# A hybrid decoder layer on one core: one store per pair for the turned head outputs, and their weaving in four copies

## The chip, the core and the metric

The kernel runs as one program on one core of a Trainium2 chip. Its engines are PE (matmuls), DVE (VectorE), ACT (ScalarE), POOL (GpSimd) and SP, which here only issues DMAs. The metric is the device time of one execution in microseconds; the median of three runs before the change is 1531.04 us.

## The reference

One layer over 1024 rows of 1024 channels, in float32: a normalised input is projected to eight groups of 1024 channels, two token mixers run side by side, gates merge them, then an output projection and an MLP with squared ReLU follow. What the change touches is the second mixer's output `o` and where it meets its gates:

```python
h = rms_norm(x, norm_mix)
proj = h @ w_in
xa, ga, q, f, v, g, m_a, m_b = split(proj)               # eight groups of 1024
y_a = rg_lru(conv(xa), ...) * gelu(ga)
o = rms_norm(hgrn2_chunkwise(silu(q), kf, log_f, v), hg_norm)   # 8 heads of 128
y_b = o * silu(g)
y = sigmoid(m_a) * y_a + sigmoid(m_b) * y_b
x = x + y @ w_out
x = x + square(relu(rms_norm(x, norm_mlp) @ w_up)) @ w_down
return rms_norm(x, norm_final)
```

## The kernel before

**Stages.** The rows are worked on in two halves of 512 (c = 0, 1), the heads in four pairs (p = 0 to 3). First come the mixers, eight stages of (c, p), up to about 545 us. Then the gates: the channel groups g, m_b, ga and m_a, computed over all rows, up to about 815 us. Then the output projection, the MLP and the final norm. Every float32 factor is split into a rounded upper part H and a lower part L (`split`: a cast on ACT makes H, a subtraction on DVE makes L), and each product is three matmuls (`mm3`, L158), so that one product of 128x512 outputs over 512 channels is 12 matmuls.

**The head outputs.** In the mixers, `on` holds a stage's normalised outputs with rows on partitions. The DMA transposition works on 16-bit halves of the float32 words, so `onT` (`on_T`) comes out with the low and the high 16-bit halves of each number apart. It is stored to DRAM (`od[p]`, one tensor per pair), by ACT's DMA queue. In the gate stage `with_o(p)` loads the pair's `od` into `op` (L1281, one DMA of 128 partitions x 8 KB), puts the two halves back together with one copy on ACT (L1282, "weaving": it reads half-planes and writes them interleaved into `o`) and multiplies `g2`, the product of gates g and m_b, by the norm's gain and `o` on DVE (L1285).

**The gate stage.** It goes in quads: q = 4p + gate, gate 0 to 3 for g, m_b, ga, m_a; quads 0 and 1 are done in the mixers' last stage, so q runs from 2 to 15. Each quad multiplies two 2x2 blocks with seven products instead of eight; (q, s) below is step s of quad q. Steps 0, 2, 4, 6 go to a bank of PSUM called X, 1 and 5 to Y, 3 to Z. A step adds onto what its bank holds, and what the bank held must first be read out: after steps 0, 1, 2 by a copy on ACT (`ge`, L1209), after 3, 4, 5 by a sum on DVE (`gb`, L1212), after 6 by a copy on ACT (`gb`, L1214):

```python
        if step < 3:
            ge[q, step] = gp.tile([P, T], F32, tag="e", name=f"ge{step}_{q}", bufs=4)
            added[q, step] = A.copy(ge[q, step], o)
```

So (q, 2) waits for the copy of (q, 0), (q, 4) for that of (q, 2), (q, 5) for that of (q, 1), (q, 6) for the sum of (q, 4). Steps 3 to 6 of a quad read operands called B21, T3, B22, T4; T3 and T4 are made in the mixers, stored in DRAM (`cdT`) and loaded as H and L parts (`gT3H`, `gT3L`, `gT4H`, `gT4L`) by SP at the start of the stage (L1176). The first two quads are interleaved: (2,0), (2,3), (2,1), (2,2), (2,5), (2,4), (3,0), (2,6), then (3,1) to (3,6), (4,0) and so on. The weights of quad q are `q` tiles of number 32 + q, loaded two DMAs per quad (`load_quad`), summed on DVE (`s`, L1121 to L1130) and split into the pairs named wA11, ws1, ws3 and wA12 (`wA`, `ws136H` for quad 4, and so on).

**What sets the order.** The engines run their instructions in order. The order is made by a scheduler from the order of writing, priorities (`tc.high_priority`) and manual edges: `held(a, b)` puts a behind b without a wait across engines, and `added[q, s]` is the instruction that read out step s of quad q. `in_turn` issues a DMA on SP with high priority, behind the last one so issued. Each DMA of SP and ACT takes the next of eight semaphores (DMAHW0 to DMAHW7) and, where that one's last user has not landed, waits for it on its queue.

**The turned keys.** In a mixer stage (`hgrn`) the keys are turned on PE into the banks `pk`, copied by ACT into `kT` (L868), and PE's next product (`pkv`) reads them.

Of the kernel before, what the change touches and what calls it, by code (L numbers as in the profile page):

```python
# [15 lines left out]
ALU = mybir.AluOpType  # L16
# [3 lines left out]
P = 128  # L20
D = 1024
S = 1024
T = 512
# [18 lines left out]
PV_LB, PV_CB, PV_BR, PV_BI, PV_LAM, PV_CW, PV_HG = 0, 8, 16, 24, 32, 40, 72  # L42
# [4 lines left out]
def trunk(ctx: ExitStack, tc: tile.TileContext, x, wts, mlp, pv, gains, mask_f, mask_u, out):  # L47
    nc = tc.nc
    V, A, G, PE = nc.vector, nc.scalar, nc.gpsimd, nc.tensor
# [39 lines left out]
    def held(ins, behind, reason="order"):  # L89
        how = mybir.DependencyInfo(mybir.DependencyClass.NoSync, mybir.DependencyReason.DATA)  # L90
        tc.add_manual_dep(ins.ins, behind.ins.name, how, reason=reason)
        return ins
# [76 lines left out]
    pvt = const.tile([P, PV_N], F32, tag="pvt", name="pvt")  # L169
# [60 lines left out]
    od = [dram.tile([P, 2, 4 * T], U16, tag=f"od{p}", name=f"od{p}") for p in range(NPAIR)]  # L230
# [327 lines left out]
    def on_T(c, p, got, queue):  # L558
        t = mt("tmp", f"onT{c}{p}", (P, 2, T)).rearrange("p a b -> p (a b)").bitcast(U16)
        t = t.rearrange("p (j x) -> p j x", x=P)  # L560
        ins = queue.dma_start_transpose(t, got["on"].rearrange("p g j d -> p (g j d)").bitcast(U16))

        turned_on.append(ins)

        def stored(dma):
            for g in range(2):
                dst = od[p][64 * g : 64 * g + 64, :, 2 * c * T : 2 * (c + 1) * T]
                src = t[:, 8 * g : 8 * g + 8, :].rearrange("p j x -> p (j x)")
                dma(dst.rearrange("a h t -> (a h) t"), src)

        return stored

# [117 lines left out]
    def hgrn(c, p, got, go):  # L690
# [117 lines left out]
        for b in range(4):  # L808
# [5 lines left out]
                op0=ALU.mult,  # L814
                op1=ALU.add,
# [4 lines left out]
        for n in range(8):  # L820
            for b in (0, 2):
                k = 4 * n + b
# [33 lines left out]
        nkv = 3 if c + 1 == NC else 4  # L856
# [3 lines left out]
        pk = [bank("hg", f"pk{c}{u}") for _, u in both]  # L860
# [3 lines left out]
        kT = []  # L864
        kTs = mt("rr", f"kT{nm}", (P, 2, 4, P))
        for s, u in both:
            kT.append(kTs[:, s])
            A.copy(kT[s][:, :nkv, :], pk[s][:, : nkv * P].rearrange("p (n k) -> p n k", n=nkv))  # L868
        go(at[3])
        pkv = [bank("hg", f"pkv{c}{u}") for _, u in both]  # L870
        for s, _ in both:
# [4 lines left out]
        for s, u in both:  # L876
            sn = sns[:, s]
            states.append([scar[:, u, :]] + [sn[:, n, :] for n in range(4)])
            for n in range(nkv):
# [3 lines left out]
                else:  # L883
# [5 lines left out]
                        op0=ALU.mult,  # L889
                        op1=ALU.add,  # L890
# [294 lines left out]
    def behind_steps(ins):  # L1185
        how = mybir.DependencyInfo(mybir.DependencyClass.NoSync, mybir.DependencyReason.DATA)
        tc.add_manual_dep(ins.ins, added[own[1], 4].ins.name, how, reason="behind_steps")
# [37 lines left out]
    def gate_work(q):  # L1225
        p, gate = divmod(q, 4)
        b = gb.pop(q)
        if gate == 0:
            sg = gp_tile("sg", f"sg{q}")
            sigmoids(sg, b)  # L1230
            V.tensor_tensor(out=b, in0=sg, in1=b, op=ALU.mult)
            live["g2"] = b
        elif gate == 1:
            sigmoids(b, b)
            V.tensor_tensor(out=live["g2"], in0=live["g2"], in1=b, op=ALU.mult)
            with_o(p)
        elif gate == 2:
            t = gp_tile("sg", f"sg{q}")
            A.activation(t, b, AF.Square)
            ins = V.tensor_scalar(t, t, 0.044715, 1.0, op0=ALU.mult, op1=ALU.add)  # L1240
            if q == own[0]:
                behind_steps(ins)
            V.tensor_tensor(out=t, in0=t, in1=b, op=ALU.mult)
            for two in (slice(0, 2), slice(2, 4)):
                ins = A.activation(t[:, two, :], t[:, two, :], AF.Tanh, scale=GELU_C)
                if q == own[0]:
                    how = mybir.DependencyInfo(mybir.DependencyClass.NoSync, mybir.DependencyReason.DATA)
                    tc.add_manual_dep(ins.ins, added[own[2], 0].ins.name, how, reason="tanh")
            for cut, one in ((slice(0, 4, 3), 1.0), (slice(1, 3), -1.0)):
                V.scalar_tensor_tensor(b[:, cut, :], t[:, cut, :], one, b[:, cut, :], op0=ALU.add, op1=ALU.mult)  # L1250
            h = load_4(hd[p], f"h{p}")
            V.scalar_tensor_tensor(b, b, 0.5, h, op0=ALU.mult, op1=ALU.mult)
            live["g1"] = b
        else:
            g1, g2 = live.pop("g1"), live.pop("g2")
            last = p + 1 == NPAIR
            yh, yl = gp_tile("sg", f"yH{p}").bitcast(F32R), gp_tile("ld", f"yL{p}").bitcast(F32R)
            for c in range(NC):
                two = slice(2 * c, 2 * c + 2)
                for j in (2 * c, 2 * c + 1):  # L1260
                    A.activation(b[:, j, :], b[:, j, :], AF.Sigmoid, scale=SIGN[j])
                ins = V.tensor_tensor(out=b[:, two, :], in0=b[:, two, :], in1=g1[:, two, :], op=ALU.mult)
                if q == own[1]:
                    held(ins, added[own[2], 4])
                for j in (2 * c, 2 * c + 1):
                    op = ALU.add if p == 0 or SIGN[j] > 0 else ALU.subtract
                    ins = V.tensor_tensor(out=b[:, j, :], in0=b[:, j, :], in1=g2[:, j, :], op=op)
                    if q == own[1]:
                        how = mybir.DependencyInfo(mybir.DependencyClass.NoSync, mybir.DependencyReason.DATA)
                        tc.add_manual_dep(ins.ins, added[own[2], 4].ins.name, how, reason="sums of the next")  # L1270
                if last and c == 0:
                    split(b[:, two, :], yt[0][p][:, 0], yt[0][p][:, 1])
                else:
                    split(b[:, two, :], yh[:, two, :], yl[:, two, :])
                    for t, y in enumerate((yh, yl)):
                        nc.sync.dma_start(yd[p][:, t, two, :], y[:, two, :].bitcast(F32))

    def with_o(p):
        parts, o = gp_tile("ld", f"op{p}"), gp_tile("sg", f"o{p}")
        as_16 = lambda t: t.rearrange("p a b -> p (a b)").bitcast(U16)  # L1280
        nc.sync.dma_start(as_16(parts), od[p].rearrange("a h t -> a (h t)"))  # L1281
        A.copy(  # L1282
            as_16(o).rearrange("p (t h) -> p h t", h=2), as_16(parts).rearrange("p (h t) -> p h t", h=2)
        )
        ins = V.scalar_tensor_tensor(  # L1285
            live["g2"], live["g2"], pvt[:, PV_HG : PV_HG + 1], o, op0=ALU.mult, op1=ALU.mult
        )
        if p == 0:
            behind_steps(ins)

    yt = {}

# [39 lines left out]
    gwork[own[0]]["c"]()  # L1332
    live["g2"] = gp_tile("b", "g2_0")
    nc.sync.dma_start(live["g2"], g2d)
    for q in own:
        n = q + 1
        if n > own[1] and n < QUADS:
            gwork[n] = quad_steps(GQ + n, (w1p, wp), minus=True)
        for step in (1, 2, 5, 4, 6) if q == own[0] else (0, 1, 2, 3, 4, 5, 6):
            if q in own[1:3] and step == 0:  # L1340
                continue
            pinned[0] = q < own[2]
            gate_step(q, step)
            if q == own[0] and step == 4:
                gate_step(own[1], 0)
            if q == own[2] and step == 4:
                gate_work(own[1])
            if q == own[1] and step == 6:
                pinned[0] = False
                gate_step(own[2], 0)  # L1350
                with_o(0)
                gate_work(own[0])
            pinned[0] = False
            if n == QUADS:
                if step == 2:
                    close_np()
                    yp, close_yp = opened("yp", side="right")
                    y_tiles(yp, 0)
                    most[0] = len(seq)
                    fill_w(n_mix + 1)  # L1360
                if step == 5:
                    fill_w(n_mix + 3)
                continue
            if step == 1 and q > own[0]:
                load_quad(GQ + n, dma=in_turn if n == own[2] else nc.sync.dma_start)
            for k in {2: ("sums", "a", "b"), 5: ("c",), 6: ("d",)}.get(step, ()):
                if (q, k) == (own[1], "sums"):
                    gwork[n][k](rest_a12)
                elif q > own[0]:
                    gwork[n][k]()  # L1370
                elif k != "a":
                    with tc.high_priority(300):
                        done = gwork[n][k]()
                    if k == "d":
                        rest_a12 = done
        if q > own[1]:
            gate_work(q)
# [572 lines left out]
```

## Time and profile before

| what | value |
|---|---|
| three runs, us | 1527.86, 1531.04, 1532.47 |
| median, us | 1531.04 |
| profiled execution, us | 1529.59 |
| its span, us | 1527.8 |
| PE / DVE / ACT / POOL busy, us | 1514.5 / 1147.3 / 811.1 / 154.5 |
| granted PE clock, mean | 0.999 |
| weaving copies on ACT (L1282), count and mean us | 4, 4.84 |
| stores of onT (od), count and size | 16, 256 KB |
| loads of op, count and size | 4, 1024 KB |

The span runs from the first to the last instruction of the profiled execution; the time has a little more around it. Busy times of engines overlap. A row of a timeline gives start and duration in us, engine, line, operation, output<-input, and in brackets how long its engine stood idle before it and what ended that. A row of the waits gives who waited for whom, the total in us, how many times, and the longest.

### The profile page before, as it was taken

The numbers are of one execution on the slowest core, as the hardware profiler recorded it, in microseconds if no ns is written. First come the engines' busy times: TensorE is split into PE (matmuls) and PEld (weight loads), VectorE is DVE, ScalarE is ACT, GpSimd is POOL, SyncE is SP. The second block draws the span as 40 slices with busy tenths as digits, with TensorE's granted clock in tenths as the row PEclk, the third lists the DMA queues.
The fourth block names the chain that finished last, engine by engine and source line by source line (L and its number), as shares of the span: only waits on it lengthen the run. The fifth ranks groups of instructions, "written<-read, shape, count | busy, mean of one in ns | idle before, by whom it ended". The sixth has DMA issues, their size and how long they took to land.

```text
span 1527.8 us, 23130 instructions
## 1 busy us (share of the span) xinstructions
PE 1514.5 (99%) x9027; PEld 1268.6 (83%) x9027; DVE 1147.3 (75%) x1661; ACT 811.1 (53%) x1333; POOL 154.5 (10%) x191
## 2 busy tenths in 40 slices
PE   9999999999999999999999999999999999999998
PEld 7888988888889878788888888888888888888886
DVE  6888686485585738786856578888888998888877
ACT  6556746656668336555553447666666722111115
POOL 1021110232633600000000000000000000000000
PEclk9999999999999999999999999999999999999999
DMA  8546456476674384332339334666666766666642
GB/s 298 199 170 217 153 198 221 143 230 220 207 240 158 110 311 156 135 137 87 134 106 331 128 111 161 259 248 251 248 250 249 253 264 264 249 249 250 250 191 110
DMA packets 100047, 311.01 MB, mean 204 GB/s; under 512 B 25313, under 2 KB 38753, under 8 KB 87010
## 3 DMA queue, kind: packets, MB, share of 16 engines
q1 hardware_dynamic: 93392, 298.91, 54.0%
q10 hardware_dynamic: 6546, 10.62, 2.0%
q8 instruction: 71, 1.16, 0.3%
q14 instruction: 38, 0.31, 0.1%
HBM read 201.50 MB, written 103.81 MB: 200 GB/s over the span
## 4 chain that ended last, share of the span: by engine, by line
PE 77%; DVE 4%; DMA 2%; ACT 1%; issue 1%; SPq 0%; DVEq 0%; ACTq 0%
PE uX L158 11%; PE dX L158 11%; PE gX L158 8%; PE po L158 6%; PE dY L158 6%; PE uY L158 6%; PE gY L158 4%; PE pj_f L158 3%; PE pv L158 3%; PE pj_q L158 3%; PE pj_xa L158 3%; PE uZ L158 3%; PE dZ L158 3%; PE gZ L158 2%; PE mb L158 1%
## 5 line engine op out<-in xcount | busy, mean ns | idle before, releaser
L1836 DVE TENSOR_TENSOR acc<-acc,dX 128x512 f32<-128x512 f32 x128 | 85.0, 683 | 26.8 <-PE dX L158 26.1
L95 ACT CAST wA<-q 128x512 fp32r<-128x512 f32 x46 | 28.6, 622 | 118.5 <-PE dX L158 94.4
L99 DVE TENSOR_TENSOR wL<-raw,wH 128x1024 fp32r<-128x1024 f32 x46 | 56.3, 1226 | 33.8 <-ACT wH L95 32.9
L158 PE MATMUL po<-wH,y 128*128 128x512 f32 x256 | 80.5, 391 | 0.0
L95 ACT CAST wH<-raw 128x1024 fp32r<-128x1024 f32 x46 | 48.2, 1049 | 35.1 <-DMA raw<-wts_in 14.8
L1736 POOL TENSOR_TENSOR gx<-acc,gain 128x256 f32<-128x256 f32 x1 | 0.7, 741 | 604.6 <-DVE acc L1836 604.6
L158 PEld LDWEIGHTS po<-wH,y 128*128 128x128 f32 x256 | 48.1, 188 | 9.8
L1836 DVE TENSOR_TENSOR acc<-acc,dY 128x512 f32<-128x512 f32 x64 | 43.6, 685 | 14.3 <-PE dY L158 13.8
L158 PE MATMUL po<-wL,y 128*128 128x512 f32 x128 | 49.8, 389 | 0.0
L1584 ACT ACTIVATE b<-b 128x512 f32<-128x512 f32 x48 | 30.0, 625 | 29.7 <-DVE b L1583 27.9
L158 PE MATMUL uX<-h2B11H,wA 128*128 128x512 f32 x128 | 42.1, 390 | 0.0
L193 POOL TENSOR_TENSOR rstd_h<-rstd_h,mhalf 128x1 f32<-128x1 f32 x8 | 4.3, 543 | 373.0 <-DVE rstd_h L188 373.0
L121 ACT CAST wH<-raw 128x1024 fp32r<-128x1024 f32 x36 | 37.2, 1045 | 7.3 <-issue 3.7
L99 DVE TENSOR_TENSOR wA<-q,wA 128x512 fp32r<-128x512 f32 x46 | 31.4, 685 | 12.8 <-ACT wA L95 12.8
L596 DVE SCALAR_TENSOR_TENSOR xc<-xp,pvt,xc 128x512 f32<-128x512 f32 x48 | 40.0, 841 | 1.2 <-ACT xc L580 1.1
L158 PE MATMUL gX<-hT00H,wA 128*128 128x512 f32 x112 | 36.8, 389 | 0.0
L502 POOL TENSOR_TENSOR stt<-r,stt 128x256 fp32r<-128x256 f32 x16 | 21.2, 1344 | 122.4 <-ACT stt L501 110.2
L1121 DVE TENSOR_TENSOR s<-q,q 128x512 f32<-128x512 f32 x46 | 31.6, 687 | 1.4 <-DMA q<-mlp_in 1.1
L1129 DVE TENSOR_TENSOR s<-q 128x512 f32<-128x512 f32 x46 | 31.5, 685 | 0.2
L905 ACT ACTIVATE on<-po 128x128 f32<-128x128 f32 x64 | 16.8, 277 | 26.1 <-PE po L901 26.0
L1585 ACT ACTIVATE b<-b 128x512 f32<-128x512 f32 x48 | 30.1, 630 | 1.0
L158 PEld LDWEIGHTS uX<-h2B11H,wA 128*128 128x128 f32 x128 | 24.0, 188 | 4.9
(2325 smaller groups left out, 5291.2 us busy)
## 6 DMA issues: line engine op xcount, KB each, us to landing
q<-mlp_in SPq DMA_DIRECT2D x92, 512.0 KB, 3.9
raw<-wts_in SPq DMA_DIRECT2D x80, 512.0 KB, 4.7
rest<-wL SPq DMA_DIRECT2D x36, 512.0 KB, 2.9
wL<-rest SPq DMA_DIRECT2D x36, 512.0 KB, 4.1
hd<-ri SPq DMA_DIRECT2D x16, 256.0 KB, 3.0
od<-onT ACTq DMA_DIRECT2D x16, 256.0 KB, 5.9
cdT<-stT SPq DMA_DIRECT2D x16, 256.0 KB, 3.1
op<-od SPq DMA_DIRECT2D x4, 1024.0 KB, 6.7
```

Source lines behind the costliest of these rows:

```text
L95: ins = casts[name] = A.copy(h, src)
L99: ins = V.tensor_tensor(out=lo, in0=src, in1=h.bitcast(F32), op=ALU.subtract)
L121: A.copy(h, raw)
L158: ins = PE.matmul(o, a, b, start=begins, stop=ends, **how)
L502: G.tensor_tensor(out=lo, in0=src, in1=h.bitcast(F32), op=ALU.subtract)
L596: ins = V.scalar_tensor_tensor(xc[:, s, :], xp[:, j : j + T], pvt[:, PV_CW + 8 * j + u : PV_CW + 8 * j + u + 1], xc[:, s, :], op0=ALU.mult ...
L905: A.activation(row(s, n), halves_of(po[s][:, n * P : (n + 1) * P]), AF.Square, accum_out=ssq[:, 4 * s + n : 4 * s + n + 1],)
L1121: ins = V.tensor_tensor(out=sa[:, 0, :], in0=a21, in1=a22, op=ALU.add)
L1129: V.tensor_tensor(out=sb[:, 0, :], in0=a21, in1=a11, op=ALU.add)
L1584: A.activation(b[:, at, :], b[:, at, :], AF.Relu, scale=-1.0 if at == 2 else 1.0)
L1585: A.activation(b[:, at, :], b[:, at, :], AF.Square)
L1836: return V.tensor_tensor(out=dst, in0=dst, in1=banks[bk, pr], op=op)
```

## The change

It has four parts. (1) `od[p]` keeps the two 16-bit halves in another place in DRAM, so that one DMA (L566 after) stores a stage's `onT` instead of two (L569 before). (2) The load is put together again on the other side: two DMAs of 64 partitions each, runs of 4 KB instead of 8 KB; for pair 0 they are issued `in_turn`, behind the loads of T4, instead of after quad 3. (3) The weaving is cut into four copies of 512 numbers per partition. For pair 0 they are held behind the copies of (3,1), twice, and (3,2), twice; for the other pairs behind those of (q+1, 0), (q+1, 1), and twice (q+1, 2), where q is the pair's m_b quad, and the product with `g2` is written after the last. (4) The copies of the turned keys get a priority.

```diff
@@ on_T
         def stored(dma):
-            for g in range(2):
-                dst = od[p][64 * g : 64 * g + 64, :, 2 * c * T : 2 * (c + 1) * T]
-                src = t[:, 8 * g : 8 * g + 8, :].rearrange("p j x -> p (j x)")
-                dma(dst.rearrange("a h t -> (a h) t"), src)
+            dma(od[p][:, :, 2 * c * T : 2 * (c + 1) * T], t.rearrange("p (g j) x -> p g (j x)", g=2))
@@ hgrn
-            A.copy(kT[s][:, :nkv, :], pk[s][:, : nkv * P].rearrange("p (n k) -> p n k", n=nkv))
+            with tc.high_priority(100):
+                A.copy(kT[s][:, :nkv, :], pk[s][:, : nkv * P].rearrange("p (n k) -> p n k", n=nkv))
@@ gate_work, gate 1
-            with_o(p)
+            spread_o(q, p)
@@ with_o
-    def with_o(p):
+    woven, due = {}, {}
+
+    def load_o(p, dma):
         parts, o = gp_tile("ld", f"op{p}"), gp_tile("sg", f"o{p}")
         as_16 = lambda t: t.rearrange("p a b -> p (a b)").bitcast(U16)
-        nc.sync.dma_start(as_16(parts), od[p].rearrange("a h t -> a (h t)"))
-        A.copy(
-            as_16(o).rearrange("p (t h) -> p h t", h=2), as_16(parts).rearrange("p (h t) -> p h t", h=2)
-        )
+        for g in range(2):
+            dma(
+                as_16(parts)[64 * g : 64 * g + 64].rearrange("p (h t) -> p h t", h=2),
+                od[p][:, g, :].rearrange("(a h) t -> a h t", h=2),
+            )
+        woven[p] = o
+
+        def piece(j, behind=None):
+            cut = slice(j * T, (j + 1) * T)
+            ins = A.copy(
+                as_16(o).rearrange("p (t h) -> p h t", h=2)[:, :, cut],
+                as_16(parts).rearrange("p (h t) -> p h t", h=2)[:, :, cut],
+            )
+            if behind is not None:
+                held(ins, behind)
+
+        return piece
+
+    def with_o(p):
         ins = V.scalar_tensor_tensor(
-            live["g2"], live["g2"], pvt[:, PV_HG : PV_HG + 1], o, op0=ALU.mult, op1=ALU.mult
+            live["g2"], live["g2"], pvt[:, PV_HG : PV_HG + 1], woven.pop(p), op0=ALU.mult, op1=ALU.mult
         )
         if p == 0:
             behind_steps(ins)
+
+    def spread_o(q, p):
+        piece = load_o(p, nc.sync.dma_start)
+        for j in range(3):
+            due[q + 1, j] = lambda j=j: piece(j, added[q + 1, j])
+
+        def last():
+            piece(3, added[q + 1, 2])
+            with_o(p)
+
+        due[q + 1, 3] = last
@@ the gate stage's loop
     nc.sync.dma_start(live["g2"], g2d)
+    piece = load_o(0, in_turn)
...
             gate_step(q, step)
+            if (q, step) in due:
+                due.pop((q, step))()
+            if q == own[1] and step in (1, 2):
+                for j in (2 * step - 2, 2 * step - 1):
+                    piece(j, added[q, step])
```

The lines of the program move by -3 to +32, so L1209 before is L1207 after, L1212 is L1210, L1214 is L1212, L1176 is L1174.

On ACT, in quads 2 and 3 of the gate stage (ge_3 are the copies of quad 3, gb<-gX the copy after a step 6, o<-op the weaving), there stands before:

```order
L95 CAST ws335H<-s_6228 128x1024
L95 CAST wA_6339<-q_6315 128x512
L95 CAST wA1235H<-q_6154 128x1024
L1214 COPY gb_6163<-gX_6162 128x512
L1209 COPY ge_3_6313<-gY_6300 128x512
L95 CAST ws136H<-s_6333 128x1024
L1209 COPY ge_3_6331<-gX_6267 128x512
L1282 COPY o_6420<-op_6419 128x2x2048
L95 CAST wA_6478<-q_6454 128x512
```

and after:

```order
L95 CAST ws335H<-s_6224 128x1024
L95 CAST wA1235H<-q_6146 128x1024
L1212 COPY gb_6155<-gX_6154 128x512
L1207 COPY ge_3_6309<-gY_6296 128x512
L1290 COPY o_6191<-op_6190 128x2x512
L1290 COPY o_6191<-op_6190 128x2x512
L1207 COPY ge_3_6329<-gX_6263 128x512
L1290 COPY o_6191<-op_6190 128x2x512 x2
L95 CAST wA_6339<-q_6313 128x512
L95 CAST ws136H<-s_6333 128x1024
```

The pieces stand around the copy of (3,2), and the first casts of quad 4's weights (wA, ws136H) have moved behind them.

On ACT, from quad 5's end to quad 6 (gb are the sigmoids of quad 5, ge_6 the copies of quad 6), before:

```order
L1218 ACTIVATE gb_6573<-gb_6573 128x512
L1282 COPY o_6701<-op_6700 128x2x2048
L95 CAST ws338H<-s_6622 128x1024
L1218 ACTIVATE gb_6573<-gb_6573 128x512
L95 CAST wA1238H<-q_6604 128x1024
L1214 COPY gb_6573<-gX_6572 128x512
L1218 ACTIVATE gb_6573<-gb_6573 128x512 x2
L1209 COPY ge_6_6719<-gX_6705 128x512
L1209 COPY ge_6_6734<-gY_6721 128x512
L95 CAST ws139H<-s_6754 128x1024
L1209 COPY ge_6_6752<-gX_6705 128x512
```

and after:

```order
L95 CAST ws338H<-s_6618 128x1024
L1216 ACTIVATE gb_6569<-gb_6569 128x512
L95 CAST wA1238H<-q_6600 128x1024
L1212 COPY gb_6569<-gX_6568 128x512
L1216 ACTIVATE gb_6569<-gb_6569 128x512
L1207 COPY ge_6_6714<-gX_6700 128x512
L1290 COPY o_6697<-op_6696 128x2x512
L1207 COPY ge_6_6730<-gY_6717 128x512
L1290 COPY o_6697<-op_6696 128x2x512
L95 CAST ws139H<-s_6752 128x1024
L1207 COPY ge_6_6749<-gX_6700 128x512
L1290 COPY o_6697<-op_6696 128x2x512 x2
```

The weaving of pair 1 has left quad 5 and stands in pieces between the copies of quad 6.

On SP, at the start of the gate stage, with the semaphores that each issue waits for (q are weights, g<-g2d the part of `g2` made in the mixers, h<-hd the first mixer's output), before:

```order
L1176 DMA gT3H<-cdT_108 128x2048 [waits DMAHW2_49]
L1176 DMA gT3L<-cdT_108 128x2048 [waits DMAHW3_49]
L1176 DMA q_6153<-mlp_in 128x1024 [waits DMAHW4_49]
L1176 DMA q_6154<-mlp_in 128x1024 [waits DMAHW5_49,DVE_49]
L1176 DMA gT4H<-cdT_109 128x2048 [waits DMAHW6_49,PE_49]
L1176 DMA gT4L<-cdT_109 128x2048 [waits DMAHW7_49]
L1176 DMA q_6315<-mlp_in 128x1024 [waits DMAHW0_49,DMAHW4_49,DVE_49,Activation_49]
L1176 DMA q_6316<-mlp_in 128x1024 [waits DMAHW1_49,DVE_49]
L1334 DMA g_0_6196<-g2d 128x2048 [waits DMAHW2_49]
L1281 DMA op_6419<-od_97 128x4096 [waits DMAHW3_49]
L1109 DMA q_6454<-mlp_in 128x1024 [waits DMAHW0_49,DVE_49,Activation_49]
L1109 DMA q_6455<-mlp_in 128x1024 [waits DMAHW5_49,DVE_49]
```

and after:

```order
L1174 DMA gT3L<-cdT_108 128x2048 [waits DMAHW3_49]
L1174 DMA q_6145<-mlp_in 128x1024 [waits DMAHW4_49]
L1174 DMA q_6146<-mlp_in 128x1024 [waits DMAHW5_49,DVE_49]
L1174 DMA gT4H<-cdT_109 128x2048 [waits DMAHW6_49,PE_49]
L1174 DMA gT4L<-cdT_109 128x2048 [waits DMAHW7_49]
L1174 DMA op_6190<-od_97 64x2x2048 [waits DMAHW0_49]
L1174 DMA op_6190<-od_97 64x2x2048 [waits DMAHW1_49]
L1174 DMA q_6313<-mlp_in 128x1024 [waits DMAHW2_49,DMAHW4_49,DVE_49,Activation_49]
L1174 DMA q_6314<-mlp_in 128x1024 [waits DMAHW3_49,DVE_49]
L1360 DMA g_0_6188<-g2d 128x2048
L1220 DMA h_6428<-hd_93 128x2048 [waits DMAHW1_49,DMAHW5_49,DMAHW0_49,Activation_49]
L1107 DMA q_6450<-mlp_in 128x1024 [waits DMAHW6_49,DMAHW2_49,DVE_49]
```

The load of op has moved ahead of quad 4's weights and of `g2`, the load of h ahead of quad 5's weights. In the built program the last user of DMAHW2, DMAHW3, DMAHW4 and DMAHW5 ahead of these rows is, before, the transposition of the last `on`, the first and the second store of it, and the last store of `g2d`; after, the first store of `g2d`, the transposition, the one store, and the last store of `g2d`. The matmuls stand in the same order in both kernels.

## The prediction

> **What bounds the kernel now.** I read the page first, then who waits for whom on PE.
>
> ```profile
> PE 1514.5 (99%) x9027; PEld 1268.6 (83%) x9027; DVE 1147.3 (75%) x1661; ACT 811.1 (53%) x1333; POOL 154.5 (10%) x191
> PE gX L158 <- ACT ge L1209: 1.4, 2, 1.0
> PE gX L158 <- DMA gT4L<-cdT: 1.2, 1, 1.2
> ...
> PE pkv L873 <- ACT kT L868: 0.3, 1, 0.3
> ```
>
> PE is busy for 99% of the span, and its order is the same, matmul for matmul, in both kernels. So the change can only take away or add waits of PE. Near the places it touches there are four: two behind bank copies (ge), one behind the load of T4's lower half, one behind the copy of the turned keys. The view counts a wait from the modelled end of the matmul before. Start to start gives the full price:
>
> ```profile
> 565.21 0.39 PE L158 MATMUL gX<-gT4H,wA1234H 128*128 128x512 f32 x1
> 566.79 0.50 PE L158 MATMUL gX<-gT4L,wA1234H 128*128 128x512 f32 x1 [1.19 <-DMA gT4L<-cdT]
> 567.12 0.40 PE L158 MATMUL gX<-gT4H,wA1234L 128*128 128x512 f32 x1
> ...
> 596.41 0.39 PE L158 MATMUL gZ<-hT01H,wA1236L 128*128 128x512 f32 x1
> 597.18 0.50 PE L158 MATMUL gX<-gT3H,ws336H 128*128 128x512 f32 x1 [0.38 <-ACT ge L1209]
> 597.51 0.40 PE L158 MATMUL gX<-gT3L,ws336H 128*128 128x512 f32 x1
> ...
> 629.91 0.39 PE L158 MATMUL gY<-gt1H,ws138L 128*128 128x512 f32 x1
> 631.33 0.50 PE L158 MATMUL gX<-gn2H,ws138H 128*128 128x512 f32 x1 [1.02 <-ACT ge L1209]
> 631.66 0.39 PE L158 MATMUL gX<-gn2L,ws138H 128*128 128x512 f32 x1
> ...
> 639.78 2.72 PE gY L158 x12
> ```
>
> The last row, from the chain that ended last, gives the undisturbed pace: a step of 12 matmuls in 2.72 us, 0.227 each. Two matmuls should take 0.45 us. They take 1.91 at T4 (loss 1.46), 1.10 at step (4,4) (loss 0.65) and 1.75 at step (6,2) (loss 1.30). The keys' wait is 0.3 by the view. These four, 3.7 us, are all that the change can win, 0.24% of the span.
>
> **The wait at (6,2), 1.30 us.** Step (6,2) adds onto the bank of (6,0), so it waits for that bank's copy on ACT:
>
> ```profile
> 622.05 4.83 ACT L1282 COPY o<-op 128x4096 uint16<-128x4096 uint16 x1 [2.29 <-DMA op<-od]
> 626.74 1.05 ACT L95 CAST ws338H<-s 128x1024 fp32r<-128x1024 f32 x1
> ...
> 630.68 0.59 ACT L1209 COPY ge<-gX 128x512 f32<-128x512 f32 x1
> ```
>
> ACT waited for the load of op, wove for 4.83 us, and a cast and four more instructions then stood in line before the copy. The matmuls of (6,0) had long ended: (6,1) ends at 629.91 + 0.23 = 630.14, so (6,0) at 627.4. In the new order no weaving stands ahead of that copy; ACT reaches it some 4.7 us sooner and is then limited by PE. The wait goes: -1.30.
>
> The four pieces now stand behind the copies of (6,0), of (6,1) and, two together, of (6,2). No row shows a piece. Its bounds are 1.05 us, the cast of as many elements in the second row, and 4.83, the whole. I take 1.2, a quarter of 4.83, since the weaving is one even pass. One piece fits between copies that come 2.72 us apart. After the last two, 2.4 us, the scaled product on DVE (L1285, 2.35 us in a row further down) follows, and then the sum of (6,4), 0.7, which must be done before (6,6). The copy of (6,2) ends about 1.75 us after its step (a 1.05 us cast stands ahead of it): 1.75 + 2.4 + 2.35 + 0.7 = 7.2 of the 8.16 us that three steps last. A margin of about 1 us covers it, in quads 10 and 14 alike; pieces of 1.7 us would use it up.
>
> **The wait at (4,4), 0.65 us.**
>
> ```profile
> 572.41 0.59 ACT L1209 COPY ge<-gY 128x512 f32<-128x512 f32 x1 [1.47 <-PE gY L158]
> 574.89 1.05 ACT L95 CAST ws136H<-s 128x1024 fp32r<-128x1024 f32 x1 [1.90 <-PE gX L158]
> 575.85 0.57 ACT L1209 COPY ge<-gX 128x512 f32<-128x512 f32 x1
> 578.55 4.84 ACT L1282 COPY o<-op 128x4096 uint16<-128x4096 uint16 x1 [2.13 <-DMA op<-od]
> 583.25 0.62 ACT L95 CAST wA<-q 128x512 fp32r<-128x512 f32 x1
> ...
> 593.22 2.01 ACT L1245 ACTIVATE sg<-sg 128x1024 f32<-128x1024 f32 x2 [2.55 <-DVE sg L1243]
> ...
> 596.54 0.58 ACT L1209 COPY ge<-gX 128x512 f32<-128x512 f32 x1
> ...
> 575.98 1.22 DVE L99 TENSOR_TENSOR ws136L<-s,ws136H 128x1024 fp32r<-128x1024 f32 x1 [0.76 <-ACT ws136H L95]
> 577.79 0.69 DVE L1212 TENSOR_TENSOR gb<-gZ,ge 128x512 f32<-128x512 f32 x1 [0.59 <-PE gZ L158]
> 580.51 0.69 DVE L1212 TENSOR_TENSOR gb<-gX,ge 128x512 f32<-128x512 f32 x1 [2.03 <-PE gX L158]
> 583.42 2.35 DVE L1285 SCALAR_TENSOR_TENSOR g<-g,pvt,o 128x2048 f32<-128x2048 f32 x1 [2.21 <-ACT o L1282]
> ...
> q<-mlp_in SPq DMA_DIRECT2D x92, 512.0 KB, 3.9
> ```
>
> The copy of (4,2) at 596.54 came late because ACT stood in the two tanh, which waited for DVE, and DVE's row of work leading there began with the product that waited for the weaving until 583.4. With the pieces behind the copies of 572.41 and 575.85, the weaving ends at about 575.8 + 0.5 + 2.4 = 578.7. What it is moved ahead of counts: the A11 cast of quad 36 (0.5 to the next start) and ws136's cast (1.05) now end at about 580.1, ws136's lower half on DVE (1.1) at 581.2, the two sums (0.6 each), which ran at 577.79 and 580.51, at 582.4. By the first of these rows (3,3) ended at 577.8, so (3,6), which needs the second sum, starts at 583.2: a margin of 0.8. The product then starts near 582.4 instead of 583.42, and the lower half of an A11 (0.6) no longer stands behind it, so the way to the tanh is about 1.6 us shorter, more than is needed: -0.65.
>
> What can be late next is the weights of quad 37: on SP the load of h now stands ahead of them and waits for the last piece, and both of their issues wait for ws136's work. Issued at about 580 and 581, at 3.9 us each and some more behind h's megabyte, they land near 585.5; their first sum is due on DVE at about 586, after one more product and cast. That is tight, but 0.9 us of the 1.6 are to spare.
>
> **The loads and the wait for T4, 1.46 us.** The load of op stands right behind T4's in the same queue; if the engines served both evenly after all, its megabyte at the rate below would cost 1.0/417 = 2.5 us, but the queue's order speaks against it. What can move T4 is the store. Two DMAs of the turned heads become one, and each DMA takes the next of eight semaphores and waits until its last user has landed:
>
> ```profile
> SPq L1176 <- DMA od<-onT: 7.2, 2, 6.9
> ...
> 552.86 0.32 SPq L1176 DMA_DIRECT2D gT3L<-cdT  x1
> ...
> 556.07 0.65 SPq L1176 DMA_DIRECT2D gT4L<-cdT  x1
> ...
> 544.00:554.00 10.00, 10.00 (x46) 8.28 (x45) 2.36 (x2) 2.72 (x4) 0.00 (x0) 1.00 1.06 339
> 554.00:557.00 3.00, 3.00 (x15) 2.49 (x14) 0.69 (x1) 0.59 (x1) 0.00 (x0) 1.00 0.86 220
> 557.00:565.00 8.00, 8.00 (x37) 6.60 (x37) 3.69 (x6) 1.21 (x2) 0.00 (x0) 1.00 1.00 417
> ...
> DMA to landing us min/median/max: 10.7/10.7/10.7
> ```
>
> SP stands 6.9 us with T3's lower half until the store has landed; T4's lower half, issued at 556.07, lands 10.7 us later (last row), at 566.7. With one DMA fewer the semaphores are dealt out differently: T3's lower half waits only for the transposition and can start some 7 us earlier. But quad 35's second half, and T4 behind it, still wait for the last g2d store. The windows' last two columns, the share of the DMA engines and GB/s, say that the engines were nearly full from 544 to 565, so T3's megabyte, moved forward, holds up the stores by as much as it spares T4 later. Bounds: at 220 instead of 417 GB/s, (417 - 220) x 3 / 417 = 1.4 us went unused, which can be won (the whole wait, -1.46) or lost once more while the queue stands empty (+1.4). Full engines with the same bytes are the nearest row: 0.
>
> The merged store saves eight issues of about 0.3 us on ACT's queue, whose waits do not reach PE there; the second load per pair costs four on SP, which mostly waits. Both: 0.
>
> **The keys' copy, 0.3 us.** The priority is to bring it ahead, but in the new order it stands after the same instructions as before: 0. The one move beside it, on DVE, puts two lower halves of h behind four small products; PE reads those halves in a much later stage: 0.
>
> Sum: -1.30 - 0.65 + 0 + 0 = -1.95 us.
>
> **The rivals.** *T4's wait goes too*: -1.95 - 1.46 = -3.4. For it speaks the 6.9 us wait that disappears, against it the full engines.
>
> *The load of op lands too late* (the slower side). In quad 3 ACT now comes to the first piece at about 573, and the copy of (3,2) stands behind two pieces. If op lands after 574.8, that copy ends after 574.8 + 2.4 + 0.6 = 577.8, when (3,4) should start, and PE loses a microsecond for each; the sums before (3,6) take about 0.9 more. Op landed like this:
>
> ```profile
> DMA to landing us min/median/max: 6.6/6.7/8.4
> ```
>
> Behind T4 (566.7), with 2.5 us for a megabyte at 417 GB/s or all of the 8.4, it lands between 569.2 and 575.1; the middle is in time. From 575.9 on the loss, 1.1 + 0.9, outweighs the gain; landing at 578.5, where it landed before, costs 3.7 + 0.9, net +2.7. The Trainium skill speaks on this side: "DMA: Bandwidth & Descriptors", Rules for kernel authors, advises against two transfers to disjoint halves of the partitions, which run one after the other on the same engines, and for one of 128 partitions. By that rule splitting the load wins nothing; no row here shows such a pair.
>
> *Nothing is won*: another instruction of the same row of work, the sums or the weights of quad 37, takes over. For it speaks DVE's 75%, against it that ACT's own line alone held the copy at 630.68. Net between 0 and -0.6.
>
> **How the numbers follow.** The profiled execution took 1529.59 us (span 1527.8 and 1.8 around it), 1.45 below the median of the three runs, 1531.04. The four executions lie within 4.6 us, 0.3%, about what a measurement of this kernel can tell from no change. Their middle is (1529.59 + 1531.04) / 2 = 1530.3. From there: forecast 1530.3 - 1.95 = 1528.4, chance 0.45; T4 too, 1526.9, 0.25; nothing won, about 1530.0, 0.18; op too late, 1533.0, 0.12. The range, 1525.6 to 1532.2, reaches from below the second case to beyond the third by about 1.3 us for the spread of executions, and leaves out most of the late load. No case moves the time by over 4.6 us, so within 0.3% gets 0.84; faster needs T4's case and a low set of runs, 0.1; slower needs op beyond 580, 0.06.
>
> **What would show it.** Right: no wait of PE for ge; four copies of 128x1024 uint16 per pair, about 1.2 us each; the bank copy of (6,0) near 627.6; the product of pair 0 before 582.6; T4's lower half still near 566.7 though T3's is issued near 546. Wrong: a wait of PE in quad 3, or for a sum (L1212) in quads 6, 10 or 14; pieces of 1.7 us; op landing after 574.8; quad 37's weights held up on SP behind h past 587.

## The result, and the profile after

The changed kernel takes 1546.4 us (median of eight runs, 1538.8 to 1553.1) against 1528.7 us before: 17.7 us between the medians. The ratio, over all runs, is 1.0107, interval 1.0083 to 1.0131, or some 16 us. The profiled execution is the fastest of the eight: 1538.82 us, span 1536.8, 9.0 more than before. First the waits of PE:

```profile
PE gX L158 <- ACT ge L1207: 7.1, 1, 7.1
PE gX L158 <- DMA gT4L<-cdT: 2.8, 1, 2.8
...
PE pkv L871 <- ACT kT L866: 0.4, 1, 0.4
```

The two waits for bank copies are gone, as forecast. A single new one for a bank copy is five times as long as both, and T4's wait has more than doubled. PE's timeline gives the place and the full price, and the windows (us, PE busy and its count, granted clock, share of the DMA engines, GB/s) the clock behind it:

```profile
553.46 0.39 PE L158 MATMUL gY<-gt1H,ws134L 128*128 128x512 f32 x1
560.97 0.79 PE L158 MATMUL gX<-gn2H,ws134H 128*128 128x512 f32 x1 [7.12 <-ACT ge L1207]
561.56 0.63 PE L158 MATMUL gX<-gn2L,ws134H 128*128 128x512 f32 x1
561.99 0.63 PE L158 MATMUL gX<-gn2H,ws134L 128*128 128x512 f32 x1
...
573.92 0.39 PE L158 MATMUL gX<-gT4H,wA1234H 128*128 128x512 f32 x1
577.06 0.50 PE L158 MATMUL gX<-gT4L,wA1234H 128*128 128x512 f32 x1 [2.75 <-DMA gT4L<-cdT]
...
560.00:565.00 5.00, 4.03 (x10) 0.50 0.95 337
565.00:573.00 8.00, 8.00 (x36) 0.99 0.84 305
```

Step (2,2), at the very start of the gate stage, waits for the copy of (2,0): 7.51 - 0.23 = 7.3 us lost. Behind it the clock is 0.50, and ten matmuls come late, most of them by 0.2 us, 2.1 us together. T4 loses 3.14 - 0.23 = 2.9 instead of 1.4. Against that the 0.65 at (4,4) and the 1.30 at (6,2) are won: 7.3 + 2.1 + 1.5 - 0.65 - 1.30 = 8.95, where the spans differ by 9.0. That the two are so close is partly luck: PE came to the stage 0.6 us earlier than before, and small differences elsewhere take about 0.7 back.

Why ACT came late to the copy of (2,0) stands in ACT's timeline, with its queue (ACTq). Before:

```profile
541.01 1.59 ACTq L561 DMA_TRANSPOSE onT<-on  x1
545.69 0.60 ACT L1044 ACTIVATE smb<-mb 128x512 f32<-128x512 f32 x1 [3.41 <-PE mb L158]
545.70 0.34 ACTq L569 DMA_DIRECT2D od<-onT  x1
546.37 0.60 ACT L1044 ACTIVATE smb<-mb 128x512 f32<-128x512 f32 x1
...
549.09 0.59 ACT L1209 COPY ge<-gX 128x512 f32<-128x512 f32 x1 [1.18 <-PE gX L158]
```

After:

```profile
540.35 5.01 ACTq L561 DMA_TRANSPOSE onT<-on  x1
545.41 0.60 ACT L1042 ACTIVATE smb<-mb 128x512 f32<-128x512 f32 x1 [3.77 <-PE mb L158]
557.47 0.54 ACTq L566 DMA_DIRECT2D od<-onT  x1
558.05 0.60 ACT L1042 ACTIVATE smb<-mb 128x512 f32<-128x512 f32 x1 [12.04 <-DMA onT<-on]
...
560.33 0.59 ACT L1207 COPY ge<-gX 128x512 f32<-128x512 f32 x1 [0.75 <-DVE g L1043]
```

The store waits for the last transposition, and ACT stands behind the store. Before, the store went out 4.7 us after the transposition's issue; after, 17.1 us. ACT stood for 12.0 us, so the second sigmoid came 11.7 us later than before, and behind it a product on DVE and then the copy of (2,0), which started 11.2 us later than before; (2,2) was due at 553.7. What ran beside the transposition is on SP. Before:

```profile
542.53 0.32 SPq L1176 DMA_DIRECT2D gn2L<-cdn  x1
545.59 0.32 SPq L1176 DMA_DIRECT2D gT3H<-cdT  x1
```

After:

```profile
539.37 0.32 SPq L1174 DMA_DIRECT2D gn2L<-cdn  x1
542.12 0.32 SPq L1174 DMA_DIRECT2D gT3H<-cdT  x1
557.46 0.32 SPq L1174 DMA_DIRECT2D gT3L<-cdT  x1
```

Before, T3's upper half waited for the semaphore that the transposition held, and n2's lower half for the one of the first store of `g2d`. With one DMA fewer the semaphores are dealt out one place on: two megabytes go out ahead of and during the transposition. T3's lower half now gets the transposition's semaphore and stands until 557.46; quad 35's weights and T4 stand behind it, which gives T4's longer wait.

### The profile page after: what moved, and what is told of

The parts are those of the page before. It is cut to its first block, busy times and chain, and to the rows that moved or that the text cites. A ratio compares the mean times of both kernels' runs of the same rounds, so it can differ in the third digit from the quotient of the medians.

```text
span 1536.8 us, 23140 instructions
## 1 busy us (share of the span) xinstructions
PE 1516.5 (99%) x9027; PEld 1269.9 (83%) x9027; DVE 1147.9 (75%) x1661; ACT 813.3 (53%) x1345; POOL 154.7 (10%) x191
## 4 chain that ended last, share of the span: by engine, by line
PE 61%; DMA 3%; DVE 1%; ACT 0%; SPq 0%; issue 0%; ACTq 0%; DVEq 0%
PE uX L158 11%; PE dX L158 11%; PE gX L158 9%; PE po L158 6%; PE uY L158 6%; PE dY L158 5%; PE gY L158 5%; PE uZ L158 3%; PE dZ L158 3%; PE gZ L158 2%; DMA onT<-on 1%; DMA gT4L<-cdT 1%; DMA acc<-x 1%; PE xT_h L1464 0%; DMA g2d<-g 0%; DVE acc L1868 0%
## 5 line engine op out<-in xcount | busy, mean ns | idle before, releaser
L903 ACT ACTIVATE on<-po 128x128 f32<-128x128 f32 x64 | 16.9, 278 | 26.1 <-PE po L899 26.0
```

Source lines behind the costliest of these rows:

```text
L903: A.activation(row(s, n), halves_of(po[s][:, n * P : (n + 1) * P]), AF.Square, accum_out=ssq[:, 4 * s + n : 4 * s + n + 1],)
```

## The experiments

Theory A: this shift of the semaphores, and nothing else in the change, costs the time. Rivals, each of which would put the cost elsewhere: B, the early load of `op` or the copies in four; C, the single store itself.

**e1, two stores again.** Everything else as changed.

```diff
-            dma(od[p][:, :, 2 * c * T : 2 * (c + 1) * T], t.rearrange("p (g j) x -> p g (j x)", g=2))
+            for g in range(2):
+                src = t[:, 8 * g : 8 * g + 8, :].rearrange("p j x -> p (j x)")
+                dma(od[p][:, g, 2 * c * T : 2 * (c + 1) * T], src)
```

> The changed kernel, with each stage's turned head outputs stored by two DMAs again (into the new places in DRAM); the early load of op, the four copies and the keys' priority stay. Theory A (with one DMA fewer the semaphores move round by one, T3's upper half and n2's lower half no longer wait behind the last transposition, their 8 KB packets run beside its 256-byte packets and it lands at 557 instead of 546; ACT stands behind the store that waits for it, PE behind ACT's bank copy): the wait of 7.1 us for ge at (2,2) and the half clock after it are gone, the transposition lands within 6 us of its issue, and the 2 us of ge waits in quads 4 and 6 stay won: 1526.7 us, 0.998 to 1.000 of before. Theory B (the early load of op, or the copies in four, disturb the stage's start): still 1540 to 1550.

1527.7 us, ratio 0.9991 (0.9983 to 1.0000). All waits for ge are gone; the loss of the change is gone, B falls. But T4:

```profile
PE gX L158 <- DMA gT4L<-cdT: 1.9, 1, 1.9
...
565.00:568.00 3.00, 1.11 (x6) 1.00 1.02 255
568.00:572.00 4.00, 4.00 (x12) 0.57 1.03 244
```

T4's lower half was issued at 556.20 and landed at 567.5 (11.3 us later), 0.8 later than before, and the clock fell behind the wait (last row; 12 matmuls in 4 us, where 0.227 us each would make 17). That was not expected.

**e2, the kernel before with one store.** Into the same places; nothing else.

```diff
-            for g in range(2):
-                dst = od[p][64 * g : 64 * g + 64, :, 2 * c * T : 2 * (c + 1) * T]
-                src = t[:, 8 * g : 8 * g + 8, :].rearrange("p j x -> p (j x)")
-                dma(dst.rearrange("a h t -> (a h) t"), src)
+            dst = od[p].rearrange("(g a) h t -> (a h) g t", g=2)
+            dma(dst[:, :, 2 * c * T : 2 * (c + 1) * T], t.rearrange("p (g j) x -> p g (j x)", g=2))
```

> The kernel before, with one edit: one DMA instead of two stores each stage's turned head outputs, into the same places in DRAM as before; load, weaving and keys as before. Theory A: the loss of the changed kernel comes with this edit alone: 1540 to 1553 us, ratio 1.008 to 1.016, with a wait of PE for ge at (2,2) of 5 us or more and the last transposition over 12 us from issue to landing; the two ge waits of quads 4 and 6 stay as well. Theory B: 1528.7 us, ratio 0.998 to 1.002.

1544.3 us, ratio 1.0098 (1.0085 to 1.0111). The waits, and the last transposition from the table of DMAs (time from issue to landing):

```profile
PE gX L158 <- ACT ge L1207: 13.2, 4, 11.3
...
onT<-on ACTq DMA_TRANSPOSE x1, 21.4
```

The loss comes with this edit alone, and the two waits of before, at (4,4) and (6,2), are there too.

**e3, the changed kernel with a spare load.** A load of 8 numbers per partition, into a tile that nothing reads (`pad_t`), takes the one semaphore that the merged store left over.

```diff
     def load_combo(o):
         for q in range(2):
+            if (o, q) == ("n2", 1):
+                in_turn(pad_t[:, 0:8], pv[:, 0:8])
             in_turn(gop[o][q].bitcast(F32), cd[o][:, q])
```

> The changed kernel, and ahead of n2's lower half on SP a load of 8 numbers per partition into a tile that nothing reads: it takes one semaphore, so that n2's lower half, T3's halves and quad 35's weights wait for the same DMAs as in the kernel before; the store stays one DMA. Theory A: 1526.7 us (0.997 to 1.001 of before), as with two stores. Theory C (the one store is itself slower, by its size, its form or its rows, and holds what stands behind it): no better than the changed kernel, 1540 to 1550. Theory B: likewise 1540 to 1550.

1530.8 us, ratio 1.0009 (1.0000 to 1.0017): the stall is gone with the single store still there, so C falls too. The 1526.7 was missed by 4: T4's wait is 2.4 us, since T3's lower half now waits for the whole 512 KB store instead of its first half (issued at 554.49; in e1 at 553.00). Behind this wait, too, matmuls come 0.2 us late each, 1.6 us in all. So the single store with its spare load has a small price of its own, 3 us against e1, which is not the 16.

```profile
PE gX L158 <- DMA gT4L<-cdT: 2.4, 1, 2.4
...
onT<-on ACTq DMA_TRANSPOSE x1, 5.7
```

**e8, the kernel before, moved round.** Here the theory is tried without any part of the change: one of the last stage's two stores goes to POOL's queue.

```diff
-        on_T(NC - 1, NPAIR - 1, gots[-1], nc.scalar)(nc.scalar.dma_start)
+        queues = [nc.scalar.dma_start, nc.gpsimd.dma_start]
+        on_T(NC - 1, NPAIR - 1, gots[-1], nc.scalar)(lambda o, i: queues.pop(0)(o, i))
```

> The kernel before, with one edit: the second of the last stage's two stores of the turned head outputs is issued on POOL's queue, which takes no semaphore of the eight. Stores, load and weaving are those of before, but n2's lower half and T3's halves now wait for the same DMAs as in the changed kernel. If the semaphores alone do it: the transposition lands over 12 us after its issue, PE waits over 5 us for ge at (2,2), 1538 to 1553 us, ratio 1.008 to 1.016. If the one store (its form or its landing) has a part in it: 1528.5 to 1533.

1544.7 us, ratio 1.0105 (1.0090 to 1.0120), as the changed kernel. T3's upper half goes out during the transposition's issue, as there, and the store that waits for the transposition 20.4 us after it:

```profile
PE gX L158 <- ACT ge L1210: 13.7, 4, 10.5
...
540.79 3.67 ACTq L561 DMA_TRANSPOSE onT<-on  x1
542.40 0.32 SPq L1177 DMA_DIRECT2D gT3H<-cdT  x1
561.18 0.36 ACTq L1051 DMA_DIRECT2D od<-onT  x1
```

**e4, the last store on POOL's queue.** This tells whether the price passes through ACT.

```diff
-        on_T(NC - 1, NPAIR - 1, gots[-1], nc.scalar)(nc.scalar.dma_start)
+        on_T(NC - 1, NPAIR - 1, gots[-1], nc.scalar)(nc.gpsimd.dma_start)
```

> The changed kernel, with the last stage's store of the turned head outputs issued on POOL's queue instead of ACT's; the other seven stay on ACT. T3's two halves now both wait for nothing that is late. Theory A, its second half (the price reaches PE only because ACT stands behind the store): the transposition still takes over 10 us from issue to landing, but ACT goes on to the bank copies, PE does not wait for ge at (2,2) and keeps its full clock; quad 35's first weights wait for the transposition, so T4 still comes late, by 1 to 4 us: 1526 to 1532 us, ratio 0.997 to 1.003. If instead PE waits for something that the transposition or the loads themselves hold up: 1538 or more.

1531.5 us, ratio 1.0012 (1.0003 to 1.0021).

```profile
PE gX L158 <- DMA gT4L<-cdT: 3.8, 1, 3.8
...
onT<-on ACTq DMA_TRANSPOSE x1, 12.2
```

The transposition is still late, but nothing on ACT waits for its landing, and the wait for ge is gone. ACT does stand in the transposition's issue, which takes 8.1 us here instead of 1.6 before, until 548.9; the copy of (2,0) still comes in time, at 553.29. What is left is T4, behind quad 35's weights, which wait for the transposition.

**e5, only T3 held back.** The spare load of e3 one place later: n2's lower half goes out at 540.06, T3's upper half waits.

> The changed kernel with the spare load put one place later, ahead of T3's upper half: T3's halves wait as in the kernel before, n2's lower half still goes out early, at about 539.5, ahead of the transposition. Tells which of the two loads does it. If T3's upper half is needed for the stall: the transposition lands 6 to 9 us after its issue, before PE comes to (2,2) at 553.7, no wait for ge; T3 and T4 come up to 3 us later than with the spare load ahead of n2: 1529 to 1533 us, ratio 1.000 to 1.003. If n2's lower half alone is enough: 1540 us or more.

1532.1 us, ratio 1.0017 (1.0007 to 1.0026).

```profile
PE gX L158 <- DMA gT3L<-cdT: 2.4, 1, 2.4
PE gX L158 <- DMA gT4L<-cdT: 1.7, 1, 1.7
...
onT<-on ACTq DMA_TRANSPOSE x1, 8.4
```

One load beside the transposition costs it about 4 us, which ACT can still take; T3's upper half is needed for the stall.

**e9, the changed kernel again**, for a second trace.

> The changed kernel once more, for a second trace. If its spread, 1539 to 1553 us, comes from how long the last transposition takes: its landing and PE's wait for ge at (2,2) differ from those of the first trace (17.1 us and 7.1 us at 1538.8 us) by about as much as the time does, half a clock behind the wait included. If the time differs and these two don't, the spread has another cause.

1544.35 us.

```profile
PE gX L158 <- ACT ge L1207: 10.1, 1, 10.1
PE gX L158 <- DMA gT4L<-cdT: 3.8, 1, 3.8
...
onT<-on ACTq DMA_TRANSPOSE x1, 20.1
...
582.00:586.00 4.00, 4.00 (x11) 0.57 1.07 180
```

Against the first trace the transposition takes 3.0 us more, the wait for ge 3.0, T4's wait about 1, and the clock now falls behind T4's wait too (8 matmuls, 0.2 us late each, 1.6): 5.6 together, where the times differ by 5.5. So between these two executions the difference in time is the difference of this transposition and what follows from it. That the whole spread, 1538.8 to 1553.1, comes from it is likely, but two traces do not show it.

**e6, op's load later**, on top of e1: between the two weight loads of quad 4, to take its megabyte away from T4. Only the main lines of the edit stand here.

```diff
-    piece = load_o(0, in_turn)
...
+            if q == own[1] and step == 1:
+                load_quad(GQ + n, dma=in_turn, mid=lambda: pieces.append(load_o(0, in_turn)))
+                piece = pieces.pop()
```

> As with two stores, and the early load of op moved from behind T4 to between the two weight loads of quad 4, which wait until about 565. If op's early load is what made T4's wait grow from 1.2 to 1.9 us and the clock fall to half behind it: the wait is 1.0 to 1.4 us again, the clock stays at 1.0, no wait for ge in quads 4 and 6, 1526.7 us, ratio 0.9980 to 0.9993. If T4's lateness has another cause: no different from two stores, 0.9991. If op now lands after 574.8, PE waits in quad 3 for (3,2)'s copy: 1528 to 1530.

1528.9 us, ratio 0.9999 (0.9989 to 1.0009). T4's lower half lands at 566.7 as before and the clock stays up, though PE, 0.5 us ahead, still waits 1.6 where 1.0 to 1.4 were expected. The rival of a late `op` came true:

```profile
575.25 2.57 ACT L1294 COPY o<-op 128x1024 uint16<-128x1024 uint16 x2 [2.27 <-DMA op<-od]
577.68 0.58 ACT L1211 COPY ge<-gX 128x512 f32<-128x512 f32 x1
...
578.32 0.50 PE L158 MATMUL gX<-gT3H,ws335H 128*128 128x512 f32 x1 [0.58 <-ACT ge L1211]
```

`op` landed at 575.2, and the copy of (3,2) behind the two copies made (3,4) wait: the prediction's late load, with its deadline of 574.8, in small.

**e7, e10, e11, both last stores and the second of g2d on POOL's queue**, with three spare loads to keep n2's lower half behind the first store of `g2d` and T3's upper half behind the transposition. T3's lower half and T4 then wait for no store. All three store by two DMAs, as e1. e7 has `op` as in e6; e10 has, besides, all four copies behind (3,2); e11 has `op` right behind T4. Only the lines that the three have to themselves stand here.

```diff
-        on_T(NC - 1, NPAIR - 1, gots[-1], nc.scalar)(nc.scalar.dma_start)
-        nc.scalar.dma_start(g2d[:, 2:4, :], g2[1])
+        on_T(NC - 1, NPAIR - 1, gots[-1], nc.scalar)(nc.gpsimd.dma_start)
+        nc.gpsimd.dma_start(g2d[:, 2:4, :], g2[1])
```

> As e6, and the last stage's two stores of the turned head outputs and its second store of g2d on POOL's queue; three spare loads of 8 numbers per partition on SP ahead of n2's lower half keep that half behind the first store of g2d and T3's upper half behind the transposition, while T3's lower half, quad 35's weights and T4 wait for no store. If T4 is late because SP stood behind the stores: T4's lower half lands before 565, its wait is gone too: 1525.2 us, ratio 0.997 to 0.9985. If T4 is late because the DMA engines are full of bytes from 544 to 565: T4's lower half lands at 565 to 567, a wait of 0.5 to 1.5 us stays, 1526 to 1527. If the loads that now go out together slow the stores or the rest of the stage's start: 1528 or more.

> As e7, with all four copies of pair 0 behind the bank copy of (3,2) instead of two ahead of it. In e7 op landed at 574.8 and (3,4) waited 1.2 us for that bank copy, since two copies that wait for op stood ahead of it. If that is so: no wait for ge anywhere, T4's wait still gone, 1526.3 us, ratio 0.9972 to 0.9986. Rival: the product with g2 and the sums behind it come later and the wait moves to (3,6) or (4,4): 1527 to 1528.

> As e7, with op's load right behind T4's as in the changed kernel. Its packets now follow T4's from about 549 on. If op's early load delays T4's lower half as in the run with two stores (by 0.8 us): it lands at about 566, PE waits 0.7 to 1.2 us for it, no wait for ge, 1526.5 to 1527.5 us. If it doesn't: no wait at all, 1525.5 to 1526.3.

e7: 1527.6 us, ratio 0.9990 (0.9980 to 1.0000). e10: 1526.9 us, 0.9990 (0.9981 to 0.9999). e11: 1528.1 us, 0.9995 (0.9984 to 1.0006). T4's lower half, issued at 548.5 in e7, landed at 565.3, and its wait is gone in all three traces, by a margin of 0.2 (e11) to 0.8 us (e10). Issued 7.6 us sooner than before, it landed only 1.4 sooner: the DMA engines were full meanwhile (a share of 0.88 to 1.03 from 546 to 565), much as the prediction had argued. The wait moved, in e7 to (3,4) (first row), in e10 to (3,6), behind a sum on DVE (second row):

```profile
PE gX L158 <- ACT ge L1211: 1.2, 1, 1.2
...
PE gX L158 <- DVE gb L1214: 1.7, 1, 1.7
```

In e11 PE waits for nothing in the gate stage. Its profiled execution took 1525.96 us, 3.6 below that of before, about what the three waits of that stage come to (1.46 + 0.65 + 1.30 = 3.4; the keys' wait stays). But it is the fastest of its eleven, and the median is only 1.3 below. All three were forecast lower: 0.997 to 0.9985 for e7, 0.9972 to 0.9986 for e10, and for e11, without a wait, 1525.5 to 1526.3 us. So the three waits can be taken away, but only 0.05 to 0.1% shows in the ratios, with 1.0 inside or at the edge of two of the three intervals. What takes back the rest is not settled: e10's profiled execution, the slowest of its twelve at 1531.71 us, has a wait of 2.6 us in the mixers, at 506.8, for DVE, with the clock at half behind it, far from all of these edits.

## Why the prediction was wrong

*The wait at (6,2): right.* The copy of (6,0) ends its wait with PE, not with the weaving:

```profile
637.05 0.59 ACT L1207 COPY ge<-gX 128x512 f32<-128x512 f32 x1 [0.70 <-PE gX L158]
637.53 1.37 ACT L1290 COPY o<-op 128x1024 uint16<-128x1024 uint16 x1
639.77 0.59 ACT L1207 COPY ge<-gY 128x512 f32<-128x512 f32 x1 [0.87 <-PE gY L158]
```

In the changed kernel this step comes 9.4 us later than before; less that, the first copy starts at 627.6, as forecast. A copy of the weaving takes 1.36 us (16 of them, 1.35 to 1.38), not the 1.2 worked out, and below the 1.7 that would have used up the margin; no sum makes PE wait in quads 6, 10 and 14.

*The wait at (4,4): right.* The product of pair 0 starts at 592.72, 13.0 us after the start of (3,1) at 579.73; before, 583.42 - 569.43 = 14.0. One us sooner was forecast, and the wait is gone. Quad 37's weights were issued at 589.89 and 591.63, in a stage 9.8 us late: near the 580 and 581 of the prediction, and no engine waited for them. The keys' copy: 0.3 before, 0.4 after, as forecast nothing.

*The loads and the wait for T4: the step that failed.* It asked what the shift of the semaphores does to T3's lower half, from 552.86 forwards, and found full engines and the same bytes: 0, with bounds of 1.4 either way. In the profiled execution the term measured 7.3 + 2.1 + 1.5 = 10.9 us of loss. It passed over the two loads ahead of it in the same row of issues. The order had it: the transposition was named as the last user of the semaphore on which T3's upper half waits, before, and the first store of `g2d` after; and T3's upper half was issued at 545.59, just ahead of the store that waited for the transposition. So T3's upper half was kept out of the transposition's way by a wait that the change took off. Its price, and n2's, is not bytes: the transposition went from 4.7 to 17.1 and 20.1 us, ACT stood behind the store, and PE behind ACT, 7.3 and 10.3 us. "The merged store saves eight issues on ACT's queue, whose waits do not reach PE there" was the second half of the same fault: they didn't, as long as the transposition took 4.7 us.

*T4 goes too*, the rival at 0.25, went the other way: T3's lower half waits only for the transposition, as the prediction said, but that landed at 557.45, so it was issued at 557.46 and not near 546.

*The load of op behind T4's, costed at 0*: in e1's trace T4's lower half took 11.3 us from issue to landing, in e6's 10.8, in e11's 17.2, in e7's 16.9: some 0.3 to 0.5 us, from one trace each. In e1's trace the clock fell behind the longer wait, but e1's median is below e6's, so no median shows the price. The rule of the Trainium skill ("DMA: Bandwidth & Descriptors", Rules for kernel authors) against splitting it in two halves was not tried by itself.

*The load of op too late*: not in the changed kernel (it landed at 582.1, ahead of the copy of (3,1) at 582.70, in a stage that ran 10 us late), but in e6 and e7, from about the landing that was worked out.

*The range.* Its upper end, 1532.2, lies 2.2 us above the third case, 1530.0, and not about 1.3 as the text there says. With 1.3 it would have been 1531.3, and the result lies far outside either.

## What to carry to other kernels

Where DMAs take semaphores in rotation, adding or dropping one DMA changes what every later one waits for; list for each of the next eight what it waited for before and what now, and ask of each wait that goes what it kept apart. A wait that looks idle may be the only thing that keeps a bulk load off a short transfer on which an engine stands. Here a spare load of 4 KB restored the rotation.

## What the hardware showed

*A transposition beside bulk loads.* From issue to landing the same transposition took 4.5 to 4.6 us with no load ahead of it and n2's half 1.8 us behind (e7, e11), 8.4 with n2's half ahead of it (e5), 17.1 to 21.4 with T3's upper half as well (the changed kernel, e9, e2). The packet records at 551.9 in the changed kernel (start in us, ns, queue, bytes; q10 is ACT's, q1 SP's) show one packet of the one for one of the other:

```
551.906  18 q10  256
551.920 309 q1  8192
552.226  18 q10  256
552.240 309 q1  8192
552.546  18 q10  256
552.560 309 q1  8192
```

A packet of the transposition takes 18 ns and then stands 0.31 us behind 8 KB. The Trainium skill ("DMA: Bandwidth & Descriptors", Queues, rings and completion order) says that each engine goes round its queues packet by packet; the trace agrees. It isn't the whole: with three loads beside it, two of them out before its issue, it took 12.2 (e4), and in the changed kernel the engines were mostly idle while it was still out:

```profile
552.00:554.00 2.00, 1.85 (x9) 1.19 (x7) 0.00 (x0) 0.00 (x0) 0.00 (x0) 1.00 0.06 23
554.00:557.00 3.00, 0.00 (x0) 0.00 (x0) 0.00 (x0) 0.00 (x0) 0.00 (x0) 1.00 0.09 39
```

A share of 0.06 to 0.09 is about one engine of 16. Why the last engines come to their part so late stays open.

*The clock.* Behind a wait of PE the clock was often at half, for 3.3 us (e1) to 5.3 us (e2), for about 4 us or ten matmuls in the changed kernel. It fell behind waits of 7.1 and 10.1 us, but also behind 2.4 (e3, e5) and 1.9 (e1), and not behind 2.8 (the changed kernel at T4). The Trainium skill ("TensorE: Matmul & The Clock Gate", Part 1) puts the fall at an idle window of about 3.4 us; in e1 it came behind a wait of 1.9 us. There the wait and the slow matmuls behind it cost 2.05 + 1.6 us, so a wait of two microseconds may cost nearly four. What decides whether the clock falls is not shown here.
